# Weight splits of the expert stage pinned in order, and copies of results issued behind the next tile's split, on one Trainium2 core

## The chip, the cores and the metric

The program runs on one core of one Trainium2 chip. The metric is device microseconds of one execution. Three executions of the kernel before took 1781.1, 1781.54 and 1781.61 us; the median is 1781.54 us.

## What is computed

A two-layer trunk over 256 tokens of width 1024, in float32. Each layer has a token mixer (RWKV-7 beside latent attention) and a channel mixer: dense SwiGLU in layer 0, and in layer 1 the part that this change touches, a top-2-of-8 expert SwiGLU with hidden width 3584:

```python
def moe_swiglu(h, router_w, router_b, w1, w3, w2):
    logits = (h @ router_w).astype(jnp.float32) + router_b.astype(jnp.float32)
    top_v, top_i = lax.top_k(logits, TOP_K)
    probs = jax.nn.softmax(top_v, axis=-1)
    combine = jnp.sum(jax.nn.one_hot(top_i, N_EXPERTS, dtype=jnp.float32) * probs[..., None], axis=-2)
    out = jnp.zeros_like(h)
    for e in range(N_EXPERTS):
        out = out + combine[..., e:e + 1].astype(h.dtype) * swiglu(h, w1[e], w3[e], w2[e])
    return out
```

## The kernel before, in words

**Split numbers.** A product of float32 matrices is made of matmuls on rounded halves: a high part (`eh` of a weight tile, a copy on ACT, line 259) and the rest (`el`, a subtraction on DVE, line 264). Where an expert has many tokens ("large": experts 0, 2, 4, 6, 7 in the kernel's order) `mm3` makes three matmuls of each block: high by high, high by low, low by high (lines 347 to 349). The three "small" experts 1, 3 and 5 (`SMALL`) hold at most 64 tokens; both halves of the tokens then lie side by side in one stationary operand, and two matmuls do (lines 1871, 1872). Of one tile in each strip of a small expert only half is split; its other half goes in as plain float32 (line 1874).

**Strips and tiles.** Each expert's hidden width is cut into 7 strips of 512 (the loop `for f in range(nf)` in `experts`). A strip takes six weight tiles of 128x2048 (1024 KB each): two of w1, two of w3, and two of w2 that belong to the strip before, since the down projection runs one strip behind. The text calls them tile 1 to tile 6 of a strip. After tile 1 come the matmuls that turn the results of the strip before (`aT`, lines 1915 and 1925), for a small expert 16 of them.

**Lead.** `Tiles.take` is called as PE comes to a tile; it issues the high part of the tile three ahead and the low part of the tile two ahead. High parts have four buffers, low parts three, so the next high part can be written when PE is done with the tile before the present one, and a low part likewise. Raw weights have ten buffers in steady state (8 `er`, and `x0`, `x1`); a buffer is given back, and the load ten tiles on is issued by SP, when its low part is made.

**Results of a small strip.** `ea` and `eb` (lines 1899 and 1900) copy the two sums out of PSUM; `aT` adds their halves and turns them; `ez` takes silu on ACT (line 1917) and multiplies on DVE (line 1918); `ealo` holds the two parts of that product (ACT line 1921, DVE line 1922), which tiles 5 and 6 of the strip multiply.

**Side work.** `step` is called eight times in a strip. It pops one piece of `todo` (router, results of the expert before), or, at every third call, one of `slow`: the gathering of the next pair of experts' tokens (`find`, `norms`, eight `gather`, `back`). What is left at the end of a pair is issued in one go.

**Who sets the order.** The code is written in program order, but a scheduler at build time orders each engine's instructions by its own estimate; only what is wrapped in `keep_in_program_order` keeps its order among itself. Before, that holds for the `aT` matmuls and for silu (1902, 1917), and not for the splits or the copies. On the chip each engine goes through its list in order.

Of the kernel before, what the change touches and what calls it, by code (L numbers as in the profile page):

```python
# [223 lines left out]
class Tiles:  # L224
# [28 lines left out]
    def splits(self, upper, lower):  # L253
        nc = self.k.nc
        while self.upper < min(upper, len(self.tiles)):
            t = self.tiles[self.upper]
            self.load(self.upper + 1)
            t[4] = self.ppool.tile([128, 2048], F32R, name="eh", tag="eh", bufs=4)
            nc.scalar.activation(t[4][:, :t[2]], t[3][:, :t[2]], AF.Copy)  # L259
            self.upper += 1  # L260
        while self.lower < min(lower, len(self.tiles)):
            t = self.tiles[self.lower]
            t[5] = self.ppool.tile([128, 2048], F32R, name="el", tag="el", bufs=3)
            nc.vector.tensor_sub(t[5][:, :t[2]], t[3][:, :t[2]], t[4][:, :t[2]].bitcast(F32))  # L264
            if t[2] == 2048:
                self.used(self.lower)
            self.lower += 1
# [54 lines left out]
class K:  # L322
# [1501 lines left out]
    def step(self, n=1):  # L1824

        for _ in range(n):
            self.calls += 1
            if self.todo:
                self.todo.pop(0)()
            elif self.slow and (n > 1 or self.calls % 3 == 0):  # L1830
                self.slow.pop(0)()
# [29 lines left out]
    def experts(self, ws, small):  # L1861
# [3 lines left out]
        nf = DFE // 512  # L1865

        def mm(ps, e, x, w, start, stop):
            if e not in small:
# [7 lines left out]
        def up(e, f, behind):  # L1876
            x, hi, lo, selT, wsl = hg[e]
            hps, n = [], 0
            for w in ("moe_w1", "moe_w3"):
                ps = self.pshh.tile([128, 512], F32, name="ph", tag="p" + w)  # L1880
                for k0 in (0, 4):
                    blocks = ws.take((w, e, f))
                    for k in range(4):
                        if k % 2 == 0:
# [9 lines left out]
                    ws.taken()  # L1894
                hps.append(ps)
            a = self.ex.tile([128, 512], F32, name="ea", tag="ea", bufs=1)
            if e in small:
                b = self.ex.tile([128, 512], F32R, name="eb", tag="eahi", bufs=1).bitcast(F32)
                act.activation(a, hps[0], AF.Copy)
                act.activation(b, hps[1], AF.Copy)  # L1900
                return a, b
            tc.keep_in_program_order(act.activation(a, hps[0], AF.Silu))
# [3 lines left out]
        def turned(now, spare=False):  # L1906
            e, f, a = now
            pt = self.pg("aT")
            if e in small:

                for i in range(2):
                    for k in range(4):
                        o = i * 256 + k * 64
                        tc.keep_in_program_order(
                            pe.matmul(pt[:, o:o + 64], a[i][:, k * 128:k * 128 + 128], self.c("sum2"), start=True, stop=True))
                z = self.work.tile([128, T], F32, name="ez", tag="sq", bufs=3)
                tc.keep_in_program_order(act.activation(z, pt[:, :T], AF.Silu))
                v.tensor_mul(z, z, pt[:, T:])
                t = self.ex.tile([128, 512], F32R, name="ealo", tag="ealo", bufs=1)
                t4, z = t.rearrange("p (k i s) -> p k i s", k=4, i=2), z.rearrange("p (k s) -> p k s", k=4)  # L1920
                act.activation(t4[:, :, 0, :], z, AF.Copy)
                v.tensor_sub(t4[:, :, 1, :], z, t4[:, :, 0, :].bitcast(F32))
                return t
# [10 lines left out]

        def down(e, f, aT, py, then=None):
            selT, wsl = hg[e][3:]
            ends, last = f == nf - 1, e == NE - 1 and f == nf - 1
            for p in range(4):
                if p % 2 == 0:
                    blocks = ws.take(("moe_w2", e, f))  # L1940
                for j in range(2):
                    c, kk = (p // 2, p % 2 * 2 + j) if ends else (j, p)
                    sl = slice(kk * 128, kk * 128 + 128)
                    x = (aT[:, sl],) if e in small else (aT[0][:, sl], aT[1][:, sl])
                    mm(py[c], e, x, blocks[p % 2 * 2 + j], f == 0 and kk == 0, ends and kk == 3)
                if then and p == 0:
                    then[2] = turned(then, True)
                if ends and p == 1:
# [203 lines left out]
```

## Time and profile before

| what | value |
|---|---|
| median of three executions | 1781.54 us |
| the profiled execution | 1786.92 us, of which the span is 1785.1 us |
| PE busy | 1660.6 us (93%) |
| DVE busy | 1460.9 us (82%) |
| ACT busy | 1124.9 us (63%) |
| data moved | 501.94 MB, mean 281 GB/s |

The expert stage fills the time from about 758 us to the end. The table is an average over stages with different limits, so the stage must be read by itself: PE's idle time there, the clock granted to it, and what it waited for. A busy PE is not PE at its peak: at the slower clock level the same matmul takes longer and counts as busy.

### The profile page before, as it was taken

Reading aid. Unit: us, or ns where it says so; the run is one execution under the profiler, and the core shown is the slowest. Engines: PE = TensorE matmul, PEld = TensorE weight load, DVE = VectorE, ACT = ScalarE, POOL = GpSimd, SP = SyncE. Lnnn points to the kernel's source line nnn. Section 1 sums busy time; section 2 is a strip of 40 time slices with the busy share of each in tenths; the row PEclk is TensorE's granted clock in tenths of the full one; section 3 lists DMA queues with packets and bytes.
Section 4 is the critical chain, followed back from the end, with each engine's and each line's share of the span. In section 5 each row is a group of like instructions: output and inputs, shape, how many; then the busy total and the mean of one; then the engine's idle time right before and its main releaser. Section 6 shows DMA issues by size and latency. Waiting matters only on the chain.

```text
span 1785.1 us, 29101 instructions
## 1 busy us (share of the span) xinstructions
PE 1660.6 (93%) x10976; PEld 1425.7 (80%) x10976; DVE 1460.9 (82%) x2085; ACT 1124.9 (63%) x1481; POOL 6.6 (0%) x19
## 2 busy tenths in 40 slices
PE   5888999999999899899998999988999888999997
PEld 4877999999998799788776788666788666888885
DVE  6897787888769688788997799866998777988986
ACT  3655556555565455567776677756777666767674
POOL 0000000000000000000000000000000000000000
PEclk9998999999999799899999999998999988999999
DMA  8734466888533556969799999888999888999990
GB/s 275 248 114 152 152 212 202 302 290 289 193 120 124 179 184 230 374 252 365 268 420 383 356 354 358 330 326 333 351 369 355 313 337 338 349 364 348 358 354 26
DMA packets 92945, 501.94 MB, mean 281 GB/s; under 512 B 11498, under 2 KB 13034, under 8 KB 49788
## 3 DMA queue, kind: packets, MB, share of 16 engines
q1 hardware_dynamic: 91788, 498.54, 75.9%
q8 instruction: 88, 1.44, 0.3%
q10 hardware_dynamic: 720, 1.42, 0.2%
q14 instruction: 61, 0.50, 0.1%
q0 software_dynamic: 288, 0.03, 0.0%
HBM read 498.91 MB, written 1.05 MB: 280 GB/s over the span
## 4 chain that ended last, share of the span: by engine, by line
PE 76%; DVE 11%; ACT 4%; issue 4%; DMA 4%; ACTq 0%; DVEq 0%
PE ph L348 7%; PE ph L347 7%; PE ph L349 7%; PE pj L347 4%; PE pj L348 4%; PE pj L349 4%; DVE el L264 4%; PE py L348 3%; PE py L349 3%; PE py L347 3%; PE ph L1872 3%; ACT eh L259 3%; PE ph L1871 2%; PE psh L347 2%; PE psh L348 2%
## 5 line engine op out<-in xcount | busy, mean ns | idle before, releaser
L264 DVE TENSOR_TENSOR el<-er,eh 128x2048 fp32r<-128x2048 f32 (+1 forms) x268 | 589.9, 2222 | 107.4 <-ACT eh L259 94.2
L259 ACT ACTIVATE eh<-er 128x2048 fp32r<-128x2048 f32 (+1 forms) x268 | 490.5, 1860 | 41.1 <-PE ph L349 16.2
L341 ACT ACTIVATE wh<-wr 128x512 fp32r<-128x512 f32 (+1 forms) x366 | 222.9, 619 | 214.1 <-PE pj L348 62.2
L342 DVE TENSOR_TENSOR wl<-wr,wh 128x512 fp32r<-128x512 f32 (+1 forms) x366 | 242.8, 673 | 66.8 <-ACT wh L341 65.5
L347 PE MATMUL pj<-hhi,wh 128*128 128x256 f32 x704 | 208.7, 303 | 9.4 <-ACT hhi L469 7.8
L348 PE MATMUL pj<-hlo,wh 128*128 128x256 f32 x704 | 203.0, 290 | 0.5 <-DVE hlo L342 0.4
L349 PE MATMUL pj<-hhi,wl 128*128 128x256 f32 x704 | 202.7, 289 | 0.0
L264 DVE TENSOR_TENSOR el<-x,eh 128x2048 fp32r<-128x2048 f32 x66 | 144.7, 2204 | 17.4 <-ACT eh L259 15.1
L347 PEld LDWEIGHTS pj<-hhi,wh 128*128 128x128 f32 x704 | 136.7, 197 | 17.0 <-ACT hhi L469 9.2
L348 PEld LDWEIGHTS pj<-hlo,wh 128*128 128x128 f32 x704 | 138.5, 197 | 2.8 <-issue 1.1
L349 PEld LDWEIGHTS pj<-hhi,wl 128*128 128x128 f32 x704 | 138.4, 197 | 1.1 <-issue 0.6
L259 ACT ACTIVATE eh<-x 128x2048 fp32r<-128x2048 f32 x66 | 120.8, 1851 | 10.9 <-PE py L349 5.6
L348 PE MATMUL py<-el,eahi 128*128 128x512 f32 x272 | 106.8, 393 | 2.9 <-DVE el L264 2.8
L349 PE MATMUL py<-eh,ealo 128*128 128x512 f32 x272 | 106.1, 390 | 0.0
L347 PE MATMUL py<-eh,eahi 128*128 128x512 f32 x272 | 102.2, 390 | 0.0
L348 PE MATMUL psh<-xu,wh 128*128 128x258 f32 x336 | 95.3, 284 | 0.0
L347 PE MATMUL psh<-xu,wh 128*128 128x258 f32 x336 | 95.2, 283 | 0.0
L349 PE MATMUL psh<-xu,wl 128*128 128x258 f32 x336 | 94.9, 282 | 0.0
L347 PE MATMUL ph<-eh,hhi 128*128 128x512 f32 x224 | 90.4, 404 | 0.0
L348 PE MATMUL ph<-el,hlo 128*128 128x512 f32 x224 | 89.0, 397 | 1.5 <-DVE el L264 1.5
L348 PE MATMUL ph<-el,hhi 128*128 128x512 f32 x224 | 88.8, 397 | 1.0 <-DVE el L264 1.0
L384 DVE SCALAR_TENSOR_TENSOR wr<-wr,cB 128x1024 f32<-128x1024 f32 x64 | 77.9, 1220 | 14.1 <-DMA wr<-in_ada_w_dram 13.8
(470 smaller groups left out, 3679.4 us busy)
## 6 DMA issues: line engine op xcount, KB each, us to landing
er<-in_moe_w_dram SPq DMA_DIRECT2D x268, 1024.0 KB, 6.9
x<-in_moe_w_dram SPq DMA_DIRECT2D x66, 1024.0 KB, 6.8
wr<-in_ada_w_dram SPq DMA_DIRECT2D x64, 512.0 KB, 4.3
wr<-in_w_in_dram SPq DMA_DIRECT2D x52, 512.0 KB, 4.1
wr<-in_ffn_up_dram SPq DMA_DIRECT2D x44, 512.0 KB, 4.3
aw<-in_ada_w_dram SPq DMA_DIRECT2D x32, 512.0 KB, 4.8
wr<-in_ffn_w_dram SPq DMA_DIRECT2D x22, 512.0 KB, 4.4
wr<-in_w_o_dram SPq DMA_DIRECT2D x16, 512.0 KB, 4.5
```

Of the source, the lines that this page charges most:

```text
L259: nc.scalar.activation(t[4][:, :t[2]], t[3][:, :t[2]], AF.Copy)
L264: nc.vector.tensor_sub(t[5][:, :t[2]], t[3][:, :t[2]], t[4][:, :t[2]].bitcast(F32))
L341: self.nc.scalar.activation(hi, src, AF.Copy)
L342: self.nc.vector.tensor_sub(lo, src, hi.bitcast(F32))
L347: mm(out, whi, xhi, start=start, stop=False, skip_group_check=True)
L348: mm(out, whi, xlo, start=False, stop=False, skip_group_check=True)
L349: mm(out, wlo, xhi, start=False, stop=stop, skip_group_check=True)
L384: x = v.scalar_tensor_tensor(w, w, 1.0, self.cB, op0=OP.mult, op1=OP.mult, accum_out=mod[:, n:n + 1])
L1871: pe.matmul(ps, x[0], w[0], start=start, stop=False, skip_group_check=True)
L1872: pe.matmul(ps, x[0], w[1], start=False, stop=stop, skip_group_check=True)
```

## The change

1. The high and low splits of expert weights are pinned: they keep program order among themselves and against everything else that is pinned on ACT or DVE.
2. For small experts a list `after` is kept. The copies `ea` and `eb`, the silu with its product (`multiplied`), and the parts of the product (`parts`) are put on it, pinned, and one of them is issued at each take of a tile, behind that take's splits. The copy of the w1 sums is now issued by itself and not together with that of the w3 sums.
3. `step` takes a piece of the gathering at every fourth call, not every third.

```diff
-            nc.scalar.activation(t[4][:, :t[2]], t[3][:, :t[2]], AF.Copy)
+            self.k.tc.keep_in_program_order(nc.scalar.activation(t[4][:, :t[2]], t[3][:, :t[2]], AF.Copy))
...
-            nc.vector.tensor_sub(t[5][:, :t[2]], t[3][:, :t[2]], t[4][:, :t[2]].bitcast(F32))
+            self.k.tc.keep_in_program_order(
+                nc.vector.tensor_sub(t[5][:, :t[2]], t[3][:, :t[2]], t[4][:, :t[2]].bitcast(F32)))
...
-            elif self.slow and (n > 1 or self.calls % 3 == 0):
+            elif self.slow and (n > 1 or self.calls % 4 == 0):
...
+        after, pin = [], tc.keep_in_program_order
+        def then():
+            if after:
+                after.pop(0)()
...
                     blocks = ws.take((w, e, f))
+                    then()
...
+                if e in small:
+                    t = (self.ex.tile([128, 512], F32R, name="eb", tag="eahi", bufs=1).bitcast(F32) if w == "moe_w3" else
+                         self.ex.tile([128, 512], F32, name="ea", tag="ea", bufs=1))
+                    hps[-1] = t
+                    after.append(lambda t=t, ps=ps: [None, pin(act.activation(t, ps, AF.Copy))][0])
+            if e in small:
+                return hps
-            if e in small:
-                b = self.ex.tile([128, 512], F32R, name="eb", tag="eahi", bufs=1).bitcast(F32)
-                act.activation(a, hps[0], AF.Copy)
-                act.activation(b, hps[1], AF.Copy)
-                return a, b
...
-                z = self.work.tile([128, T], F32, name="ez", tag="sq", bufs=3)
-                tc.keep_in_program_order(act.activation(z, pt[:, :T], AF.Silu))
-                v.tensor_mul(z, z, pt[:, T:])
...
-                act.activation(t4[:, :, 0, :], z, AF.Copy)
-                v.tensor_sub(t4[:, :, 1, :], z, t4[:, :, 0, :].bitcast(F32))
+                def multiplied():
+                    z = self.work.tile([128, T], F32, name="ez", tag="sq", bufs=3)
+                    z4 = z.rearrange("p (k s) -> p k s", k=4)
+                    pin(act.activation(z, pt[:, :T], AF.Silu))
+                    pin(v.tensor_mul(z, z, pt[:, T:]))
+                    def parts():
+                        pin(act.activation(t4[:, :, 0, :], z4, AF.Copy))
+                        pin(v.tensor_sub(t4[:, :, 1, :], z4, t4[:, :, 0, :].bitcast(F32)))
+                    after.append(parts)
+                after.append(multiplied)
                 return t
...
                     blocks = ws.take(("moe_w2", e, f))
+                    then()
```

**ACT, the sixth strip of expert 1.** Ahead stands the order before, from the copy `ea` of the strip's w1 sums (`ph_11582`). The four `eh` rows between it and `eh_11659` belong to tiles 4, 5 and 6 of the same strip and tile 1 of the next; `eh_11659` of 128x1024 is the half split of tile 2, `eh_11673` is tile 3.

```order
L1899 ACTIVATE ea_11655<-ph_11582 128x512
L259 ACTIVATE eh_11583<-er_11439 128x2048
L1917 ACTIVATE ez_11608<-aT_11599 128x256
L259 ACTIVATE eh_11614<-er_11457 128x2048
L1921 ACTIVATE ealo_11611<-ez_11608 128x4x64
L259 ACTIVATE eh_11627<-er_11484 128x2048
L1900 ACTIVATE eb_11656<-ph_11626 128x512
L259 ACTIVATE eh_11641<-er_11486 128x2048
L259 ACTIVATE eh_11659<-er_11515 128x1024
L259 ACTIVATE eh_11673<-er_11528 128x2048
```

The same place in the order now, from the high part of the strip's tile 3 (`eh_11570`) on; tiles 4, 5 and 6 are `eh_11583`, `eh_11609` and `eh_11626`, tile 1 of the next strip is `eh_11642`.

```order
L259 ACTIVATE eh_11570<-er_11424 128x2048
L259 ACTIVATE eh_11583<-er_11440 128x2048
L259 ACTIVATE eh_11609<-er_11456 128x2048
L1933 ACTIVATE ez_11615<-aT_11599 128x256
L259 ACTIVATE eh_11626<-er_11484 128x2048
L1937 ACTIVATE ealo_11608<-ez_11615 128x4x64
L259 ACTIVATE eh_11642<-er_11486 128x2048
L1909 ACTIVATE ea_11624<-ph_11582 128x512
L259 ACTIVATE eh_11658<-er_11510 128x1024
L1909 ACTIVATE eb_11657<-ph_11625 128x512
```

Before, the copy of `ph_11582` stands ahead of the high parts of that strip's tiles 4, 5 and 6. Now it stands behind all of them and behind tile 1 of the next strip. On DVE the order of such a strip is the same in both programs.

**DVE, the router at the entry of the expert stage**, before: from the comparison of the logits (line 1637) on to the ranks and what is made of them.

```order
L1637 TENSOR_TENSOR cmp_9942<-cmp_9942,eq_9943 128x128
L1638 TENSOR_REDUCE rank_9937<-cmp_9942 128x16
L1639 TENSOR_SCALAR ind_9938<-rank_9937 128x16
L1659 TENSOR_SCALAR oh0_9967<-rank_9937 128x16
L1659 TENSOR_SCALAR oh1_9968<-rank_9937 128x16
```

And now (the lines have moved down by one):

```order
L1638 TENSOR_TENSOR cmp_9942<-cmp_9942,eq_9943 128x128
L343 TENSOR_TENSOR ht1_9499<-xgT_9847,ht0_9498 128x2x256
L265 TENSOR_TENSOR el_9908<-er_9878,eh_9902 128x2048
L265 TENSOR_TENSOR el_9912<-er_9880,eh_9904 128x2048
L1639 TENSOR_REDUCE rank_9937<-cmp_9942 128x16
L343 TENSOR_TENSOR rsh_9941<-rs_y_9921,rsh_9941 128x2
```

Two low parts now stand between the comparison and the ranks. Before, the first three low parts stood further up, among the last weight splits of the token mixer.

**DVE, the end of expert 0**, where the rest of the gathering is issued in one go (`hg` on the left of line 1789 is a gathered block in PSUM; line 1796 makes the two experts' low parts), before, from the half split of tile 2 of expert 1's first strip:

```order
L264 TENSOR_TENSOR el_10972<-x1_10729,eh_10952 128x1024
L264 TENSOR_TENSOR el_11035<-er_10757,eh_10970 128x2048
L1789 TENSOR_TENSOR hg_10915<-hg_10915,rsb_10548 128x192
L1789 TENSOR_TENSOR hg_10995<-hg_10995,rsb_10548 128x192
L1796 SCALAR_TENSOR_TENSOR hlo_10546<-hg_10915,mod11_7670,hlo_10546 128x64
L1796 SCALAR_TENSOR_TENSOR hlo_10546<-hg_10995,mod11_7670,hlo_10546 128x64
L1796 SCALAR_TENSOR_TENSOR hg_10547<-hg_10915,mod11_7670,hg_10547 128x128
L1796 SCALAR_TENSOR_TENSOR hg_10547<-hg_10995,mod11_7670,hg_10547 128x128
L264 TENSOR_TENSOR el_11051<-er_10784,eh_11033 128x2048
```

And now:

```order
L265 TENSOR_TENSOR el_10953<-x1_10713,eh_10933 128x1024
L1790 TENSOR_TENSOR hg_10914<-hg_10914,rsb_10548 128x192
L1797 SCALAR_TENSOR_TENSOR hlo_10546<-hg_10914,mod11_7670,hlo_10546 128x64
L1790 TENSOR_TENSOR hg_10976<-hg_10976,rsb_10548 128x192
L1797 SCALAR_TENSOR_TENSOR hg_10547<-hg_10914,mod11_7670,hg_10547 128x128
L1797 SCALAR_TENSOR_TENSOR hlo_10546<-hg_10976,mod11_7670,hlo_10546 128x64
L1797 SCALAR_TENSOR_TENSOR hg_10547<-hg_10976,mod11_7670,hg_10547 128x128
L1790 TENSOR_TENSOR hg_10995<-hg_10995,rsb_10548 128x192
L1797 SCALAR_TENSOR_TENSOR hlo_10546<-hg_10995,mod11_7670,hlo_10546 128x64
L1790 TENSOR_TENSOR hg_10976<-hg_10976,rsb_10548 128x192
L1797 SCALAR_TENSOR_TENSOR hg_10547<-hg_10995,mod11_7670,hg_10547 128x128
```

Five gathers are left at this place where three were, and no split stands among them.

## Rows read from the trace of the kernel before

**Rows 1.** The page: span, busy time and count of instructions of each engine, and in 40 slices the clock granted to PE (tenths of full speed) and the busy share of the DMA engines.

```profile
span 1785.1 us, 29101 instructions
PE 1660.6 (93%) x10976; PEld 1425.7 (80%) x10976; DVE 1460.9 (82%) x2085; ACT 1124.9 (63%) x1481; POOL 6.6 (0%) x19
...
PEclk9998999999999799899999999998999988999999
DMA  8734466888533556969799999888999888999990
```

**Rows 2.** Busy time by stretch, core 0, cut at the start of each strip's `aT` matmuls in expert 1, with two strips at the edges of experts 3 and 5. Columns: the stretch, its length, busy us (x instructions) of PE, PEld, DVE, ACT, POOL, granted clock, DMA share, GB/s.

```profile
898.41:915.37 16.96, 16.29 (x83) 12.75 (x82) 16.09 (x18) 13.05 (x13) 0.00 (x0) 1.00 1.01 421
915.37:929.01 13.64, 13.64 (x65) 10.73 (x64) 13.64 (x9) 12.20 (x10) 0.00 (x0) 1.00 1.01 419
929.01:943.67 14.66, 13.64 (x64) 10.54 (x63) 12.17 (x9) 10.04 (x9) 0.00 (x0) 1.00 1.01 419
943.67:962.31 18.64, 15.77 (x65) 11.49 (x64) 13.07 (x9) 11.84 (x10) 0.00 (x0) 0.91 1.01 418
962.31:981.47 19.16, 15.77 (x65) 11.57 (x64) 12.87 (x9) 11.84 (x10) 0.00 (x0) 0.91 0.89 338
981.47:1000.99 19.52, 16.85 (x69) 12.20 (x68) 13.91 (x9) 14.13 (x11) 0.00 (x0) 0.91 0.90 340
1142.92:1162.07 19.15, 16.75 (x82) 12.33 (x81) 16.69 (x17) 12.88 (x11) 0.00 (x0) 1.00 0.85 335
1495.02:1515.39 20.37, 17.91 (x69) 13.49 (x68) 14.06 (x9) 14.26 (x11) 0.00 (x0) 0.83 0.87 321
```

**Rows 3.** The same view over whole small experts (four strips of expert 1, six each of experts 3 and 5), and over parts of large ones.

```profile
929.01:1000.99 71.98, 62.02 (x260) 45.80 (x259) 52.01 (x33) 47.86 (x40) 0.00 (x0) 0.93 0.95 376
1142.92:1257.99 115.07, 98.23 (x406) 71.92 (x405) 82.46 (x57) 74.29 (x62) 0.00 (x0) 0.91 0.88 333
1400.16:1515.39 115.23, 98.04 (x405) 72.06 (x404) 82.60 (x57) 74.46 (x62) 0.00 (x0) 0.91 0.88 333
...
1300.00:1400.00 100.00, 98.61 (x461) 80.50 (x460) 88.40 (x77) 73.29 (x67) 0.00 (x0) 1.00 0.93 352
1700.00:1720.00 20.00, 20.00 (x91) 16.46 (x90) 17.78 (x11) 15.14 (x10) 0.00 (x0) 1.00 0.96 360
```

**Rows 4.** ACT in order of time in expert 1's sixth strip: start, length, line, operation, count, and in brackets the idle time before and who ended it.

```profile
966.94 0.60 ACT L1899 ACTIVATE ea<-ph 128x512 f32<-128x512 f32 x1 [6.09 <-PE ph L1874]
967.43 1.90 ACT L259 ACTIVATE eh<-er 128x2048 fp32r<-128x2048 f32 x1
```

**Rows 5.** PE in order of time behind it.

```profile
969.39 0.50 PE L1871 MATMUL ph<-eh,hlo 128*128 128x512 f32 x1 [0.63 <-ACT eh L259]
971.72 0.79 PE L1872 MATMUL ph<-el,hlo 128*128 128x512 f32 x1 [1.82 <-DVE el L264]
972.31 0.63 PE L1871 MATMUL ph<-eh,hlo 128*128 128x512 f32 x1
972.74 0.63 PE L1872 MATMUL ph<-el,hlo 128*128 128x512 f32 x1
...
975.01 0.39 PE L1872 MATMUL py<-el,ealo 128*128 128x512 f32 x1
975.24 0.40 PE L1871 MATMUL py<-eh,ealo 128*128 128x512 f32 x1
...
979.76 0.50 PE L1872 MATMUL ph<-el,hlo 128*128 128x512 f32 x1 [0.93 <-DVE el L264]
```

**Rows 6.** ACT in order of time in expert 1's third strip, the one of 13.64 us.

```profile
918.04 1.91 ACT L259 ACTIVATE eh<-er 128x2048 fp32r<-128x2048 f32 x1 [0.36 <-PE ph L1871]
919.99 0.60 ACT L1899 ACTIVATE ea<-ph 128x512 f32<-128x512 f32 x1
920.49 0.41 ACT L1921 ACTIVATE ealo<-ez 128x256 fp32r<-128x256 f32 x1
921.43 2.90 ACT L259 ACTIVATE eh<-er 128x2048 fp32r<-128x2048 f32 x2 [0.54 <-ACT ealo L1921]
```

**Rows 7.** Groups of instructions by shape in 943.67 to 1000.99 us: line, engine, operation, names, shape, count, busy us, mean ns of one, idle before and who ended it.

```profile
L264 DVE TENSOR_TENSOR el<-er,eh 128x2048 fp32r<-128x2048 f32 x14 | 31.9, 2287 | 17.5 <-ACT eh L259 17.4
L259 ACT ACTIVATE eh<-er 128x2048 fp32r<-128x2048 f32 x14 | 26.4, 1904 | 0.0
...
L1922 DVE TENSOR_TENSOR ealo<-ez,ealo 128x256 fp32r<-128x256 f32 x3 | 1.3, 417 | 0.0
```

**Rows 8.** The waits of the whole run: who waited for whom, us in total, times, longest.

```profile
ACT ea L1899 <- PE ph L1874: 81.7, 14, 7.4
```

**Rows 9.** The same for the DMA queue's own waits, which is SP's.

```profile
SPq L246 <- DVE el L264: 478.7, 205, 22.7
```

**Rows 10.** The page's issues of DMAs: count, KB each, median us from issue to landing.

```profile
er<-in_moe_w_dram SPq DMA_DIRECT2D x268, 1024.0 KB, 6.9
```

**Rows 11.** DVE in order of time at the entry of the expert stage.

```profile
739.50 2.28 DVE L264 TENSOR_TENSOR el<-er,eh 128x2048 fp32r<-128x2048 f32 x1
741.70 0.41 DVE L416 TENSOR_TENSOR sqs<-sqs,sq 128x256 f32<-128x256 f32 x1
742.04 0.47 DVE L750 SCALAR_TENSOR_TENSOR xT<-pj,hg,xT 128x256 f32<-128x256 f32 x1
...
748.93 0.29 DVE L1637 TENSOR_TENSOR cmp<-cmp,eq 128x128 f32<-128x128 f32 x1
749.26 0.29 DVE L1638 TENSOR_REDUCE rank<-cmp 128x16 f32<-128x128 f32 x1
```

**Rows 12.** DVE in order of time at the end of expert 0: two gathers.

```profile
879.95 0.62 DVE L1789 TENSOR_TENSOR hg<-hg,rsb 128x192 f32<-128x192 f32 x2
880.69 0.55 DVE L1796 SCALAR_TENSOR_TENSOR hlo<-hg,mod,hlo 128x64 fp32r<-128x64 f32 x2
881.41 0.62 DVE L1796 SCALAR_TENSOR_TENSOR hg<-hg,mod 128x128 fp32r<-128x128 f32 x2 [0.17 <-ACT hg L1795]
```

More of the change, by code (lines that the diff above doesn't have):

```diff
@@ L1915, in turned @@
                             pe.matmul(pt[:, o:o + 64], a[i][:, k * 128:k * 128 + 128], self.c("sum2"), start=True, stop=True))
-                z = self.work.tile([128, T], F32, name="ez", tag="sq", bufs=3)
-                tc.keep_in_program_order(act.activation(z, pt[:, :T], AF.Silu))
-                v.tensor_mul(z, z, pt[:, T:])
                 t = self.ex.tile([128, 512], F32R, name="ealo", tag="ealo", bufs=1)
-                t4, z = t.rearrange("p (k i s) -> p k i s", k=4, i=2), z.rearrange("p (k s) -> p k s", k=4)
-                act.activation(t4[:, :, 0, :], z, AF.Copy)
-                v.tensor_sub(t4[:, :, 1, :], z, t4[:, :, 0, :].bitcast(F32))
+                t4 = t.rearrange("p (k i s) -> p k i s", k=4, i=2)
+                def multiplied():
[8 more added lines that the diff above has]
+                after.append(multiplied)
                 return t
@@ L1933, in turned, with down @@
             return ahi, alo
-        def down(e, f, aT, py, then=None):
+        def down(e, f, aT, py, other=None):
             selT, wsl = hg[e][3:]
@@ L1945, in down @@
                     mm(py[c], e, x, blocks[p % 2 * 2 + j], f == 0 and kk == 0, ends and kk == 3)
-                if then and p == 0:
-                    then[2] = turned(then, True)
+                if other and p == 0:
+                    other[2] = turned(other, True)
                 if ends and p == 1:
```

## The prediction, written before the changed kernel ran

> **What bounds the kernel now.** Read the page first: PE is busy for 93% of the span, but the clock line has 9s in its right half, where the expert stage lies, and the DMA line 9s and 8s there [rows 1]. So PE, the DMA engines and a wait are all candidates, and the stage must be cut up. The second view is busy time by stretch, one strip to a row. In large experts PE is busy for 20.00 of 20 us at full clock, although DMA runs at 360 GB/s [rows 3]: PE bounds them, and nothing there can be gained by order. In small experts a strip takes 18.6 to 19.5 us, PE is busy for some 15.8 of it, DVE for 13, ACT for 12, the clock is 0.91 and DMA moves 338 GB/s [rows 2]. No engine is full. Yet the third strip of expert 1, with the same work, took 13.64 us at clock 1.00, and DMA moved 419 GB/s [rows 2]. The loss of some 5 us per strip is a wait.
>
> The third view, the engines in order of time, names it. ACT sat idle for 6.09 us until the plain matmuls of tile 2 ended, then made the copy `ea`, and only then the high part of tile 4 [rows 4]. PE, through with tile 3, waited 0.63 us for that high part and 1.82 us for the low part that DVE made of it; later 0.93 us more [rows 5]. And the matmuls behind those gaps start 0.43 us apart (972.31, 972.74), those further on 0.23 (975.01, 975.24) [rows 5]: the lower clock level, 1.2 GHz instead of 2.4. The wait of `ea` for line 1874 happened 14 times, 81.7 us in all [rows 8]. Buffers for three more high parts were free meanwhile, but ACT goes through its list in order, and `ea` stood in front.
>
> **The change, part by part.**
>
> *Copies behind the splits.* Now `ea` stands behind the high parts of tiles 4, 5, 6 and the next tile 1. In the strip of 13.64 us the order was nearly that: `ea` stood behind tile 6's high part, and did not hold ACT up [rows 6]. That strip is my model, and I ask what is late next in it. PE's four tiles from tile 3 to tile 6 are 32 matmuls at 0.23 us, 7.3 us. Between the end of tile 2 and that of tile 6 DVE must make the low part of tile 5, the product's part, the low parts of tile 6 and of the next tile 1: 3 x 2.29 + 0.42 = 7.3 us [rows 7], a little less where splits follow each other directly (31.9 us for 14 is 2.28 each). So DVE is level with PE, and I take 13.9 us, not 13.64, per strip; the strip before the change of expert holds a first tile of a large expert with four matmuls more, 0.9 us, so 14.8; the first strip of a small expert has the old expert's results to fold in and DVE busy for over 16 us, so 17, as 16.96 shows [rows 2]. ACT has five high parts at 1.9 us and a half one, and 2 us of copies, 11.8 of 13.9: free.
>
> The sum, from the stretches of whole experts [rows 3]: expert 1, 71.98 - (3 x 13.9 + 14.8) = 15.5; expert 3, 115.07 - (17 + 4 x 13.9 + 14.8) = 27.7; expert 5, 115.23 - 87.4 = 27.8. Together 71 us. Bounds: with 13.64 per strip 4 us more, and 2 more if the first strips take 16; with half of each loss coming back as another wait, 35.
>
> *Waits that pinning adds.* `ea` now waits behind a high part that needs PE to be done with tile 3; its reader, `aT`, comes four tiles later, 7 us. `eb` follows a half split and has two tiles. Silu and the parts stand behind high parts whose buffers PE frees before `aT` ends or just after tile 2. The readers of the parts come with tile 5. I cost these at nothing; their cover is the tiles named, and without it each would cost one tile, 1.8 us.
>
> *Loads.* SP's list of loads is unchanged, and SP is released by low parts: 205 waits for DVE [rows 9]. A faster strip therefore asks for its loads sooner: 6 x 1.049 MB in 13.9 us is 453 GB/s, more than the 418 to 421 that the saturated rows show [rows 2]. At 419 a strip's loads take 15.0 us, so the queue falls behind by 1.1 us a strip, 7.7 us over seven. A load has nine tiles, 20.8 us, between its issue and its split, and lands in 6.9 [rows 10]: 13.9 us of room. It fits; cost nothing, bound below.
>
> The Trainium skill (DMA: Bandwidth & Descriptors, section "Where 436 GB/s comes from") says that for loads from HBM the memory's share of about 358 GB/s per core binds and not the ports; that would give 17.6 us per strip and speaks against this change. The rows differ: 418 to 421 GB/s stood for four strips, 64 us, with no other core of the chip in use by this program.
>
> *Entry.* Two low parts of 2.29 us now stand between the comparison (748.93) and the ranks (749.26) [rows 11], on the chain router, places, gather, first matmul: 4.5 us. The old place at 739.50 held up the last residual sums until 742.04, though PE was just done: some 1.3 us come back. The third low part moves behind the gathers, 2.3 us, half of it hidden. So 4.5 us lost; bounds 2 and 7.
>
> *Gathers at every fourth place.* Expert 0 is left with two gathers more to issue at once. A pair holds DVE for 0.62 + 0.55 + 0.62 = 1.8 us [rows 12]; the same work leaves the strips before, which PE bounds. I take 1.5 us lost, bounds -1 and +4. In the later large experts 48 calls less the results' six give ten pieces of 13 or 11: the gathers nearly all fit.
>
> *Large experts.* PE bounds them; pinning can only add. Per strip DVE has six low parts and three short results, 15 of 16.9 us. I cost it at nothing; see the last rival.
>
> Sum: 71 - 4.5 - 1.5 = 65 us. The profiled execution took 1786.92 us and would take 1721.9; the median of the runs is 5.4 us below the profiled one, so **1716.5 us** against 1781.54. With the bounds of the small terms, 1702 to 1732.
>
> **The rivals.**
>
> *A new wait in the small strips.* DVE is level with PE by my own count, and any late high part shows in full, with the lower clock behind it. For: DVE was busy for 13.64 of 13.64 us in the model strip [rows 2]. Against: the next strip, 14.66, ran into the old order again, not into DVE. At 16 us a strip, fifteen strips lose 2.1 each, 32 us: 1748.
>
> *The loads.* If DMA holds only 365 GB/s, about what it moves in large experts (352 to 360 [rows 3]), a strip takes 17.2 us. Expert 1 would use up its room and lose 9, experts 3 and 5 some 18 each, since large strips of 16.9 to 18 us hardly refill it: 45 us back, 1761. For: the DMA share is 0.93 and 0.96 there, near full. Against: SP waited for buffers in those rows, and the same queue gave 419 when asked. The skill's 358 would end in the same place.
>
> *Slower.* One mechanism: in a large strip a pinned low part stands before a short result that PE needs, or behind one that waits, and comes one split late. The price is 2.2 us in each of 35 large strips, 77 us, against 65 gained: 1793. It decides from 1.9 us a strip. Against: low parts run two tiles ahead, 5.5 us there.
>
> That the change does not do what it says can be left out: the order shows `ea` moved.
>
> **How the numbers follow.** My forecast has 0.70, the new wait 0.15, the loads 0.10, slower 0.04, other small outcomes 0.01. The range is the forecast's own 1702 to 1732, widened to 1750 to take in most of the new-wait case; it leaves out the loads, the slower case and a tail on either side, 2 in 10. About 0.2% (3.6 us) is what a measurement of this kernel can tell from no change. Faster takes the first three cases less a part of the loads, 0.94; no change 0.02; slower 0.04.
>
> **What would show it.** Right: the wait of `ea` for line 1874 gone from the list of waits; small strips of 13.6 to 14.5 us at clock 1.00 with DMA near 419 GB/s; PE's waits for low parts in the middle of small strips gone; the ranks some 4.5 us after the comparison. Wrong: a wait of `eh` for a load (loads), DVE without idle time and PE waiting for it in small strips (new wait), PE idle in large strips (slower), or small strips still at 18 us.

## The result, and the profile after

The changed kernel took 1729.19 us, median of three executions (1725.53 to 1730.41), against 1781.54 us. The ratio is 0.9702, with a 95% interval of 0.9679 to 0.9725. The profiled execution took 1730.41 us, its span is 1728.6 us; the profile before had 1785.1 [rows 1]. Forecast were 1716.5 us and a range of 1702 to 1750. All medians and ratios here leave out one slow execution, of the run pins (4078.94 us).

Start with the page again: busy time of the engines, the clock granted to PE and the DMA share in 40 slices.

```profile
span 1728.6 us, 29096 instructions
PE 1631.4 (94%) x10976; PEld 1411.1 (82%) x10976; DVE 1461.1 (85%) x2085; ACT 1123.6 (65%) x1481; POOL 6.6 (0%) x19
...
PEclk9999999999989999989999999999999999999998
DMA  8725466788733556868979999989999899999980
```

The work is the same (PE 10976 matmuls, DVE and ACT busy for as long as before). PE is busy for 29 us less with the same matmuls: more of them ran at the higher clock (1.00 in the small strips below, 0.91 in [rows 2]). The other 27 us were idle time of PE.

The busy time by stretch, cut at the same places as before: expert 1's six strips, then the first and a middle strip of expert 3, then whole small experts (the last four strips of expert 1, all six of experts 3 and 5), then a piece of a large one. Columns: the stretch, its length, busy us (x instructions) of PE, PEld, DVE, ACT, POOL, granted clock, DMA share, GB/s.

```profile
906.91:926.14 19.23, 16.62 (x82) 12.59 (x81) 17.36 (x18) 14.70 (x14) 0.00 (x0) 1.00 0.90 346
926.14:939.86 13.72, 13.72 (x65) 10.73 (x64) 13.72 (x9) 11.99 (x11) 0.00 (x0) 1.00 0.99 388
939.86:953.57 13.71, 13.71 (x65) 10.73 (x64) 13.18 (x9) 11.96 (x11) 0.00 (x0) 1.00 0.96 383
953.57:966.93 13.36, 13.36 (x64) 10.62 (x63) 12.64 (x9) 11.77 (x10) 0.00 (x0) 1.00 1.01 420
966.93:980.52 13.59, 13.59 (x65) 10.81 (x64) 12.90 (x9) 11.82 (x11) 0.00 (x0) 1.00 1.01 421
980.52:995.02 14.50, 14.50 (x69) 11.56 (x68) 13.81 (x9) 12.74 (x11) 0.00 (x0) 1.00 1.01 419
1137.61:1157.83 20.22, 17.79 (x81) 13.64 (x80) 18.10 (x18) 14.49 (x13) 0.00 (x0) 0.92 0.85 333
1171.43:1185.01 13.58, 13.58 (x65) 10.81 (x64) 12.88 (x9) 11.82 (x11) 0.00 (x0) 1.00 1.00 416
...
939.86:995.02 55.16, 55.16 (x260) 43.72 (x259) 52.53 (x33) 48.29 (x40) 0.00 (x0) 1.00 1.00 411
1137.61:1226.69 89.08, 86.65 (x406) 68.44 (x405) 83.50 (x58) 74.49 (x62) 0.00 (x0) 0.98 0.95 383
1369.39:1458.42 89.03, 86.59 (x405) 68.42 (x404) 83.13 (x58) 74.46 (x62) 0.00 (x0) 0.98 0.95 383
1660.00:1680.00 20.00, 20.00 (x91) 16.50 (x90) 17.77 (x10) 15.04 (x11) 0.00 (x0) 1.00 0.97 377
```

Read it against [rows 2, 3]. The strips of 18.6 to 19.2 us are strips of 13.4 to 13.7 now, the last strip of expert 1 went from 19.52 to 14.50, PE is busy all through them, and the clock column says 1.00. The last four strips of expert 1 went from 71.98 to 55.16 us, experts 3 and 5 from 115.07 and 115.23 to 89.08 and 89.03. The first strips had no part in the gain: 19.23 against 16.96 in expert 1, 20.22 against 19.15 in expert 3.

ACT in order of time in the strip at 1171.43 shows why, beside [rows 4]:

```profile
1175.92 0.40 ACT L1937 ACTIVATE ealo<-ez 128x256 fp32r<-128x256 f32 x1
1177.72 1.92 ACT L259 ACTIVATE eh<-er 128x2048 fp32r<-128x2048 f32 x1 [1.40 <-issue]
1179.55 0.58 ACT L1909 ACTIVATE ea<-ph 128x512 f32<-128x512 f32 x1
```

`ea` waits for nothing: the plain matmuls of tile 2 that it needs (now line 1882) ended 3.5 us before it starts. It stands behind a high part, where before it stood in front of one and waited for 6.09 us. For the 1.40 us that ACT waits before that high part the profile names no releaser; PE has no idle time in this strip. No wait of `ea` for line 1882, the old line 1874 of [rows 8], is left in the list.

Now the two places where time was lost. DVE at the entry, to be read beside [rows 11], and then in the first strip of expert 3:

```profile
749.88 0.29 DVE L1638 TENSOR_TENSOR cmp<-cmp,eq 128x128 f32<-128x128 f32 x1
...
750.69 4.48 DVE L265 TENSOR_TENSOR el<-er,eh 128x2048 fp32r<-128x2048 f32 x2
755.09 0.28 DVE L1639 TENSOR_REDUCE rank<-cmp 128x16 f32<-128x128 f32 x1
...
1146.85 2.28 DVE L265 TENSOR_TENSOR el<-er,eh 128x2048 fp32r<-128x2048 f32 x1
1149.04 0.41 DVE L1934 TENSOR_TENSOR ez<-ez,aT 128x256 f32<-128x256 f32 x1
1149.38 0.87 DVE L2008 SCALAR_TENSOR_TENSOR xT<-sct,mod,xT 128x256 f32<-128x256 f32 x2
1150.16 0.41 DVE L1938 TENSOR_TENSOR ealo<-ez,ealo 128x256 fp32r<-128x256 f32 x1
```

Two low parts stand between comparison and ranks, as forecast. In the first strip silu ended at 1142.50, but its product `ez` stands behind low parts and additions to xT and comes at 1149.04. ACT (first row) waits for it, and PE (second row) for what comes of it:

```profile
1149.49 0.42 ACT L1937 ACTIVATE ealo<-ez 128x256 fp32r<-128x256 f32 x1 [5.19 <-DVE ez L1934]
1150.62 0.50 PE L1879 MATMUL py<-eh,ealo 128*128 128x512 f32 x1 [2.05 <-DVE ealo L1938]
```

**Where the 56.5 us of span went.** From the first `aT` of expert 0 to the last `aT` of the stage: 980.29 us before (779.04 to 1759.33), 917.85 after (785.00 to 1702.85), 62.4 less. From the comparison to the first `aT`: 30.11 before, 35.12 after, 5.0 more. The comparison itself began 0.95 us later (749.88 against 748.93). 62.4 - 5.0 - 0.95 = 56.5.

### The profile page after: what moved, and what is told of

Its sections match the earlier page's. It is cut to its first block, busy times and chain, and to the rows that moved or that the text cites. A ratio compares the mean times of both kernels' runs of the same rounds, so it can differ in the third digit from the quotient of the medians.

```text
span 1728.6 us, 29096 instructions
## 1 busy us (share of the span) xinstructions
PE 1631.4 (94%) x10976; PEld 1411.1 (82%) x10976; DVE 1461.1 (85%) x2085; ACT 1123.6 (65%) x1481; POOL 6.6 (0%) x19
## 4 chain that ended last, share of the span: by engine, by line
PE 80%; DVE 10%; DMA 4%; issue 3%; ACT 2%; DVEq 0%; SPq 0%; ACTq 0%
PE ph L348 7%; PE ph L349 7%; PE ph L350 7%; PE pj L348 4%; PE pj L349 4%; PE pj L350 4%; PE py L349 4%; PE py L350 4%; PE ph L1880 3%; PE ph L1879 3%; PE py L348 3%; PE psh L348 2%; PE psh L349 2%; PE psh L350 2%; DVE el L265 2%
## 5 line engine op out<-in xcount | busy, mean ns | idle before, releaser
L265 DVE TENSOR_TENSOR el<-er,eh 128x2048 fp32r<-128x2048 f32 (+1 forms) x268 | 586.1, 2220 | 26.1 <-ACT eh L259 14.9
L385 DVE SCALAR_TENSOR_TENSOR wr<-wr,cB 128x1024 f32<-128x1024 f32 x64 | 78.0, 1219 | 17.6 <-DMA wr<-in_ada_w_dram 17.5
```

The costliest lines, as they stand in the source:

```text
L385: x = v.scalar_tensor_tensor(w, w, 1.0, self.cB, op0=OP.mult, op1=OP.mult, accum_out=mod[:, n:n + 1])
```

## The experiments

"Stage" is the time from the first `aT` to the last, "entry" from the comparison to the first `aT`, "strip" a middle strip of expert 3. Ratios are against the kernel before, run on the same chip.

| run | median us | ratio, 95% interval | entry | strip | stage |
|---|---|---|---|---|---|
| before | 1781.54 | 1 | 30.11 | 18.6 to 19.5 | 980.29 |
| changed | 1729.19 | 0.9702, 0.9679 to 0.9725 | 35.12 | 13.58 | 917.85 |
| again | 1727.04 | 0.9694, 0.9665 to 0.9723 | 35.19 | 13.59 | 917.63 |
| copies | 1731.96 | 0.9718, 0.9690 to 0.9745 | 29.81 | 14.85 | 926.43 |
| pins | 1814.44 | 1.0178, 1.0145 to 1.0210 | 35.19 | 20.4 | 1002.97 |
| eaonly | 1754.50 | 0.9839, 0.9815 to 0.9862 | 35.17 | 15.46 | 947.60 |
| prodonly | 1787.53 | 1.0025, 1.0005 to 1.0045 | 34.96 | 18.4 to 20.4 | 984.19 |
| fourth | 1788.12 | 1.0031, 1.0011 to 1.0051 | 30.15 | 18.4 to 19.4 | 982.51 |
| third | 1726.72 | 0.9703, 0.9677 to 0.9728 | 35.16 | 13.58 | 918.57 |
| raw5 | 1740.50 | 0.9775, 0.9749 to 0.9800 | 35.86 | 13.6 to 15.3 | 928.22 |
| both | 1722.59 | 0.9663, 0.9646 to 0.9680 | 30.34 | 13.59 | 916.52 |
| spread | 1716.85 | 0.9632, 0.9610 to 0.9655 | 30.35 | 13.58 | 913.33 |
| best | 1717.45 | 0.9642, 0.9607 to 0.9677 | 30.74 | 13.58 | 910.74 |

**Copies moved, splits not pinned (copies).**

```diff
-            self.k.tc.keep_in_program_order(nc.scalar.activation(t[4][:, :t[2]], t[3][:, :t[2]], AF.Copy))
+            nc.scalar.activation(t[4][:, :t[2]], t[3][:, :t[2]], AF.Copy)
...
-            self.k.tc.keep_in_program_order(
-                nc.vector.tensor_sub(t[5][:, :t[2]], t[3][:, :t[2]], t[4][:, :t[2]].bitcast(F32)))
+            nc.vector.tensor_sub(t[5][:, :t[2]], t[3][:, :t[2]], t[4][:, :t[2]].bitcast(F32))
```

> The changed kernel with the two pins on the expert weights' splits taken back; copies, silu and parts stay behind the next tile's split, gathers stay at every fourth place. Theory (the copy of the w1 product at the head of ACT's row was the block, and moving the copies alone takes it away): the strips of the small experts stay at 13.6 us, and the entry, where two low parts now run ahead of the rank, gets its 6 us back, so 1729 - 6 = about 1723 us. Rival (the splits have to be held in order for the copies to fall behind them): strips back at 17 to 19 us, 1760 to 1785 us.

The entry came back in full, 29.81 us. The strips did not stay at 13.6: 14.85. So the theory holds for the larger part (53.9 of the 62.4 us of the stage) and fails for a smaller one. DVE in order of time in a strip of this run shows it; the last row is PE's, in order of time:

```profile
1185.05 2.29 DVE L264 TENSOR_TENSOR el<-er,eh 128x2048 fp32r<-128x2048 f32 x1
1187.26 0.42 DVE L1933 TENSOR_TENSOR ez<-ez,aT 128x256 f32<-128x256 f32 x1
...
1190.83 0.42 DVE L1937 TENSOR_TENSOR ealo<-ez,ealo 128x256 fp32r<-128x256 f32 x1
...
1191.30 0.50 PE L1878 MATMUL py<-eh,ealo 128*128 128x512 f32 x1 [0.94 <-DVE ealo L1937]
```

Silu ended at 1184.40, but a low part had been moved ahead of the product. With pins the product came 0.5 us after silu (1173.75 to 1174.26). The pins on the splits thus hold the product's place: 8.6 us over the stage, of which the entry takes 5 back. By their times alone this kernel and the changed one cannot be told apart.

**Splits pinned, copies not moved (pins).** The kernel before with the two pins alone; the diff is the one above with its signs turned.

> The kernel before with the two pins on the splits alone: copies, silu and parts at their old place, gathers at every third place. In a strip of a small expert the copy of the w1 product then stands behind the splits of tiles 3 and 4 but ahead of those of tiles 5 and 6. Theory (how far the splits are ahead when ACT stops is what counts): tile 5 is split from the end of tile 2 on, copy 0.6 + part 0.4 + high part 1.9 + low part 2.3 = 5.2 us against 4.5 us of matmuls of tiles 3 and 4, so 0.7 to 1.5 us are lost a strip over the 15 strips that follow a first one: 1729 + 10 to 22, less 4 for the gathers, is 1735 to 1750 us. Rival (the copies' own move is the cause, the pins only cost): 1781 + 6 at the entry = about 1787 us.

Both theories missed: 1814 us, slower than before by 1.8%. The copy of the w1 sums had not fallen behind tile 4's high part, as the expectation took it to have; ACT stands at it for 6.00 us as before. What changed is what the scheduler then did with PE's matmuls. ACT (one row) and PE in order of time:

```profile
1220.38 0.60 ACT L1900 ACTIVATE ea<-ph 128x512 f32<-128x512 f32 x1 [6.00 <-PE ph L1875]
...
1222.83 0.50 PE L1872 MATMUL ph<-eh,hhi 128*128 128x512 f32 x1 [0.63 <-ACT eh L259]
1225.81 1.22 PE L1872 MATMUL py<-eh,ealo 128*128 128x512 f32 x2 [2.47 <-ACT eh L259]
1226.83 0.64 PE L1873 MATMUL ph<-el,hhi 128*128 128x512 f32 x1
```

Two matmuls of tile 5 (`py`) stand in the middle of tile 4 (`ph`), wait there for tile 5's high part, and hold up seven matmuls of tile 4. This wait came 12 times, 28.0 us. A pin also moves what is not pinned.

**One of the two groups moved (eaonly, prodonly).** With the splits pinned, only the two result copies stay behind the splits, or only silu, product and parts.

The first diff is that of eaonly, the second that of prodonly.

```diff
-                    pin(act.activation(z, pt[:, :T], AF.Silu))
-                    pin(v.tensor_mul(z, z, pt[:, T:]))
+                    act.activation(z, pt[:, :T], AF.Silu)
+                    v.tensor_mul(z, z, pt[:, T:])
-                    def parts():
-                        pin(act.activation(t4[:, :, 0, :], z4, AF.Copy))
...
-                    after.append(parts)
+                    act.activation(t4[:, :, 0, :], z4, AF.Copy)
...
-                after.append(multiplied)
+                multiplied()
```

```diff
-                    after.append(lambda t=t, ps=ps: [None, pin(act.activation(t, ps, AF.Copy))][0])
             if e in small:
+                for t, ps in zip(hps, pss):
+                    act.activation(t, ps, AF.Copy)
                 return hps
```

> The changed kernel with silu, product and the product's two parts back where they were (emitted with aT, not pinned); the two copies of the results stay behind the next tile's split and the splits stay pinned. Theory (the copy of the w1 product was the block; silu and parts have a whole tile of slack at either place): strips of 13.6 to 14.9 us, 1729 to 1748 us. Rival (silu and the parts in front of a split block ACT as much as the copy did): strips of 16 us or more, 1765 us or more.

> The changed kernel with the two copies of the results back in one place at the end of the w3 product and not pinned; silu, product and parts stay behind the next tiles' splits, the splits stay pinned. It is the fourth corner beside the changed kernel (13.6 us a strip), the run eaonly (15.5) and the run pins (20.4). Theory (each of the two waits stops ACT by itself: the copy of the w1 product costs 4 to 5 us a strip, silu's wait for aT 1.9 us): strips of 17.5 to 19 us, 1729 + 15 x 4 to 5.4 us = 1789 to 1810 us. Rival (the two waits overlap, and one of them gone is most of the gain): 15 to 16 us, 1750 to 1765 us.

With the copies alone a strip takes 15.46 us, between the two theories. ACT in order of time in that run:

```profile
1174.88 0.38 ACT L1933 ACTIVATE ez<-aT 128x256 f32<-128x256 f32 x1 [3.84 <-PE aT L1926]
1175.16 1.91 ACT L259 ACTIVATE eh<-er 128x2048 fp32r<-128x2048 f32 x1
```

Silu now stops ACT in front of a high part until `aT` is done: 20 times, 70.0 us in all. It costs 1.9 us a strip: PE waits there for two low parts, 0.46 and 0.32 us, and is busy for 14.59 us instead of 13.58 at the same granted clock of 1.00; where this 1.0 us arises was not followed further. With silu and parts alone moved, the wait of the w1 copy is back and the strip takes 18.4 to 20.4 us, longer than the 17.5 to 19 expected, although the run as a whole (1787.53 us) came out just below the time expected. The list of waits of that run, to be read beside [rows 8]:

```profile
ACT ea L1912 <- PE ph L1882: 83.3, 14, 7.4
```

So there are four corners with the splits pinned. The stage takes 1003.0 us with neither group moved (gathers at every third place there, which is worth nothing in the changed kernel, see third), 984.2 with the product's, 947.6 with the copies', 917.9 with both. The copy of the w1 sums was the block; silu stood behind it as a second one of about half the price (29.7 us of the stage, against 66.3). The Trainium skill (PSUM — Partial Sum Buffer, section "Engine vs sequencer instructions") says that ScalarE's queue is strict first in, first out; both waits agree, 6.09 us in [rows 4] and 3.84 us here, each with a high part right behind it that starts without a wait of its own.

**Gathers (fourth, third).** The kernel before with `self.calls % 4`, and the changed one with `self.calls % 3`, one character each.

> The kernel before with gathers at every fourth place instead of every third, nothing else. Theory (the gathers' place matters only where they run out into the border between experts 0 and 1): the border grows by about 4 us, nothing else moves: 1782 to 1787 us. Rival (a quarter fewer gathers in front of DVE's low parts gives expert 0 its time back): expert 0 shorter by 1 to 3 us and no longer border, 1778 to 1781 us.

> The changed kernel with gathers at every third place again. Theory: the border between experts 0 and 1 and the strip behind it get back the 4.2 and 2.3 us by which they grew, or most of it, and expert 0 loses its 1.7 us: 1729 - 3 to 5 = 1724 to 1726 us. Rival (the border is longer because of the pinned low parts, not of the number of gathers that are left): 1728 to 1731 us.

Compare expert 0 with the border and expert 1's first strip: before 136.33 us (779.04 to 915.37), fourth 140.30 (778.51 to 918.81), after 141.14, third 140.00 (779.75 to 919.75). In the kernel before, the later gathers cost 4.0 us there, as expected, and 2.2 us of the whole stage (982.51 against 980.29). In the changed kernel earlier gathers give back 1.1, not 4 to 6, and the stage as a whole nothing (918.57 against 917.85). The rival of the second run is right by these stretches (its median, 1726.72, lies between the two forecasts): with pinned splits the stretch is longer at either place of the gathers. The run pins, with the gathers at every third place and the copies where they were, takes 140.50 there (787.55 to 928.05). So the pins alone cost some 4 us, the later gathers alone cost some 4 us, and the two do not add up. Which pinned instruction is at fault, these runs do not say; in the run both, with the first three splits free, it is still 140.02.

**Room for the loads (raw5).**

```diff
-RAW = 8
+RAW = 5
```

> The changed kernel with 5 buffers of its own for raw weights instead of 8, so that a load has 6 tiles instead of 9 between its issue and its split: 6 x 2.27 - 6.9 = 6.7 us of room against a lag of 1.1 us a strip. Theory of the prediction (the room covers a queue that is behind by 1.1 us a strip): expert 1 as now, the last one or two strips of experts 3 and 5 lose some 1 us each, 1729 + 0 to 5 us. Rival (the 9 tiles are needed, because a load takes longer than 6.9 us when the queue is full): strips of small experts go to 15 us (6.29 MB at 419 GB/s) from the third strip on, 11 strips x 1.4 us = 15 us: about 1744 us, with waits of the high part for a load in the list.

The truth lay between. The stretches of expert 3's fourth and fifth strips in that run, with the columns of above:

```profile
1182.93:1198.21 15.28, 14.19 (x66) 10.65 (x64) 13.05 (x8) 11.67 (x10) 0.00 (x0) 1.00 1.01 421
1198.21:1213.18 14.97, 14.20 (x65) 10.65 (x64) 13.09 (x8) 12.09 (x11) 0.00 (x0) 1.00 1.01 419
```

One row of ACT in the fifth; the high parts behind it wait in the same way (46 such waits in the run, 26.1 us):

```profile
1199.32 1.92 ACT L259 ACTIVATE eh<-er 128x2048 fp32r<-128x2048 f32 x1 [0.58 <-DMA er<-in_moe_w_dram]
```

Experts 3 and 5 kept 13.6 us up to the third strip, and the fourth and fifth took 15.0 to 15.5: 6.29 MB at 419 GB/s are 15.0 us. The room exists and is used up, but sooner than I reckoned. A strip of 13.59 us falls behind by 1.4 us, not 1.1, and a load lands later the fuller the queue is. The page's DMA issues, asked for 1171 to 1226 us of the changed kernel, give 14.7 us from issue to landing, against 6.9 over the whole run before [rows 10]:

```profile
er<-in_moe_w_dram SPq DMA_DIRECT2D x21, 1024.0 KB, 14.7
```

With six tiles, 6 x 2.27 = 13.6 us, that does not fit. With nine it does, but the median hides how closely: between 1171 and 1231 us the landing climbs from 6.7 to 18.7 us. Here is one load of the changed kernel near the end of expert 3, as SP issues it, its time to landing, and the high part that ACT makes of it:

```profile
1209.60 0.33 SPq L246 DMA_DIRECT2D x<-in_moe_w_dram  x1
DMA to landing us min/median/max: 16.4/16.4/16.4
1226.88 1.91 ACT L259 ACTIVATE eh<-x 128x2048 fp32r<-128x2048 f32 x1
```

From issue to split it has 17.3 us, not 9 x 2.27 = 20.4, and it lands 0.9 us before it is needed. The closest load of expert 5 (issued at 1441.34, landed after 16.5, split at 1458.62) has 0.7 us. So no strip of the changed kernel waits for a load, but at the end of experts 3 and 5 it is less than 1 us from doing so; runs with 6 or 7 buffers were not made.

**Versions beyond the change (both, spread), and the changed kernel once more beside the last one (again, best).** In both, the first three splits are not pinned and the gathers are at every third place. spread also puts the four pieces `back` at every second call; best does that only before expert 1 and the large experts.

The first diff is that of both, the second that of spread against both; best has `self.spaced = 0 if e in (2, 4) else 4`.

```diff
+            x = nc.scalar.activation(t[4][:, :t[2]], t[3][:, :t[2]], AF.Copy)
+            if self.upper > 2:
+                self.k.tc.keep_in_program_order(x)
...
+            if self.lower > 2:
+                self.k.tc.keep_in_program_order(x)
...
-            elif self.slow and (n > 1 or self.calls % 4 == 0):
+            elif self.slow and (n > 1 or self.calls % 3 == 0):
```

```diff
             if self.todo:
-                self.todo.pop(0)()
+                if n > 1 or len(self.todo) != self.spaced or self.calls % 2 == 0:
+                    self.todo.pop(0)()
+                    self.spaced = min(self.spaced, len(self.todo)) if self.spaced else 0
...
                     self.todo.append(lambda kk=kk: back(e, kk, y, selT))
+                self.spaced = 4
```

> The changed kernel with gathers at every third place again and with the first three splits of the expert stage unpinned. Theory (two pinned low parts between comparison and ranks are the 6 us by which the entry grew, and the gathers' place is worth 4 or less): first aT at 779 instead of 785, 1726.7 - 6 = 1720 to 1721 us. Rival (the low parts have to be made before the first matmul at any place, so the entry takes as long): 1726 to 1727 us.

> The kernel of the run labelled both, with the four pieces that add an expert's results to xT put at every second place of the next expert's strips instead of at four places in a row. Theory (in the first strip of a small expert DVE is full, 17.6 of 20.2 us and the low parts late because of eight additions of 0.48 us; two of the four move into the next strip, where DVE has 0.8 us idle): the first strips of experts 3 and 5 go from 20.2 to 18.5 to 19.5 us and the second ones from 13.6 to 14.3, 1719 to 1721 less 1 to 2 us = 1718 to 1720 us. Rival (PE's own 17.8 us there and the strip behind it, where DVE is as full, give nothing): the same as both within 1 us; or 2 us slower, if the pieces collide with the product's parts.

> The changed kernel once more, beside the next run on one chip. The stages before the experts took 740 to 752 us in the profiled executions so far, by the clock; from the comparison to the first aT every kernel with the pins took 35.1 to 35.9 us and every one without 29.8 to 30.4. Expected: 1727 to 1731 us, 35.1 us from the comparison to the first aT, 917.9 us from there to the last aT.

> The kernel of the run spread, with the results put at every second place only where the next expert is expert 1 or a large one, since in experts 3 and 5 the first strip took 20.35 us with it and 19.14 without. Theory: first strips of experts 3 and 5 back at 19.1 us, 2 x 1.2 us less than spread, 911 us from the first aT to the last instead of 913.3, about 1714 to 1716 us, and some 13 us less than the changed kernel beside it. Rival (what spread gained came from the earlier stages' clock alone, 770 us to the first aT against 775): as the run both, 916.5 us from the first aT to the last, 1720 us or more.

Unpinning three splits gives the entry back (30.34 against 30.11 before), so the pins of the first splits are its cause. The run spread gained, but not where it was meant to: in the first strips of experts 3 and 5 PE waits for `ealo` as long as before. The gain lies in expert 1's first strip, 17.08 us for 19.23, and where a small expert gives way to a large one. Two stretches there, of again and then of best:

```profile
984.69:1008.73 24.04, 23.88 (x116) 19.54 (x114) 20.71 (x17) 15.42 (x13) 0.00 (x0) 1.00 1.01 420
1008.73:1019.10 10.37, 9.85 (x49) 7.67 (x48) 9.25 (x10) 8.29 (x6) 0.00 (x0) 1.00 1.01 417
```

```profile
988.46:1002.49 14.03, 14.03 (x71) 11.85 (x70) 11.27 (x8) 8.85 (x9) 0.00 (x0) 1.00 1.01 421
1002.49:1021.49 19.00, 19.00 (x93) 15.59 (x92) 18.43 (x17) 13.14 (x10) 0.00 (x0) 1.00 1.01 419
```

That is 34.4 us against 33.0, and so at all three such places; expert 1's second strip gives 0.5 us back (14.19 in spread, 13.71 in both). best stands at 19.13 us in the first strips of experts 3 and 5 where spread had 20.35, as expected in size, but the reason is not shown: both runs have the same wait there (2.07 and 2.08 us), and only the granted clock differs (1.00 and 0.92). From the comparison to the last `aT` again takes 952.8 us, both 946.9, spread 943.7, best 941.5. So by this stretch spread and best beat the changed kernel. By the whole run spread's interval lies below both of the changed kernel's, while that of best (up to 0.9677) overlaps the one of again (from 0.9665); between spread and best the medians tell nothing.

## Why the prediction was right, and where it was off

**What bounds, and the block: right.** The wait named in advance was the main cause: with everything else of the change in place, putting the copies back costs 66 us of the stage (prodonly, 984.2 against 917.9), and moving copies, silu and parts without the pins brings 53.9.

**Small strips: right in sum, wrong in two sizes.** Forecast 71 us, measured 16.8 + 26.0 + 26.2 = 69.0. The middle strips were better than 13.9, PE fills them, and DVE has 0.7 us idle of 13.58; so PE and not DVE binds. The first strips of experts 3 and 5 were put at 17 us and took 20.2. That the sum is so near is luck: the other strips gave 4.4 us more than forecast, the two first strips 6.4 us less. The model for them was expert 1's 16.96 [rows 2], a strip of the old order; in the new one it takes 19.23 itself. The step that failed is "DVE busy for over 16 us, so 17": busy time says nothing of the order, and the product stands behind three low parts and four additions. Nor was there a block to take away: before, `ea` did not wait in that strip of 19.15 us:

```profile
1149.14 0.58 ACT L1899 ACTIVATE ea<-ph 128x512 f32<-128x512 f32 x1
```

PE's idle time in it is 2.4 us before (19.15 - 16.75) and after (20.22 - 17.79); the 1.1 us more come with the granted clock, 0.92 against 1.00.

**Entry: right.** 5.0 us against 4.5. The 1.3 us that were to come back ahead of the comparison cannot be seen: there the profiled executions differ by more than that (last section).

**Gathers: mis-sized.** Forecast 1.5 us with a bound of 4, measured 4.8 (141.14 against 136.33). By fourth the gathers alone make 4.0 in the kernel before, but by third they are worth 1.1 in the changed one, and the pins alone make as much (pins, 140.50). The term that was missing is a cost of the pins at this border.

**Loads: right in the outcome, by a margin that was luck.** The forecast left 13.9 - 7.7 = 6.2 us of room. Landing climbed from 6.7 to 18.7 us around the end of expert 3, by 12 us and not 7.7, and issue to split is 17.3 us there and not 20.8; 0.9 us was left, and 0.7 in expert 5. The rate held: 416 to 421 GB/s where the queue is full. The Trainium skill (DMA: Bandwidth & Descriptors, section "Where 436 GB/s comes from") names about 358 GB/s as what binds; the measurement decides against it for one core by itself. The rival of the loads was wrong in its rate and a near one all the same: raw5 waits for loads at 419 GB/s, for want of buffers, with a price of 10 us.

**Waits that pinning adds, and large strips: right for this change only.** PE waits for nothing new in middle strips. In the first strips of experts 3 and 5 it does: the product that was put behind the next splits comes so late that ACT waits 5.19 us and PE 2.05, where the prediction put this term at nothing. The product's moved place is enough for that, without the pins on the splits: the run copies has the same wait (2.07 and 2.05 us), and in eaonly, where silu, product and parts stayed at their old place, PE waits for them nowhere. The large experts 2, 4, 6 and 7 lost 1.7 us in all, not 77. But the cost of a pin is not nothing by itself: without the moved copies the pins made the kernel slower by some 33 us. My slower rival had the place wrong (large strips); the case nearest to it sits in the small ones.

**The sum and the conversion.** Forecast 65 us off the profiled execution, measured 56.5. The 8.5 between them: small strips 2.0, entry 0.5, gathers 3.3, large experts and expert 1's second strip 1.8, the time before the comparison 0.95. The step from the profiled execution to the median was 5.4 us before and is 1.2 after, which makes 4.2 more; together they are the 12.7 us by which 1716.5 was too low. This last step is chance, since it depends on which execution was profiled. The ends 1702 and 1732 do not follow from the bounds beside the terms: those of entry and gathers give 1711.5 to 1721.5, with the strips' 6 us more 1705.5, and half of each loss coming back some 1752. By the bounds of the small terms 1729 lies outside; the end of 1732, which the working does not give, covers it. One reading is loose, without weight in the sum: as ACT's wait begins, tiles 1, 2 and 3 hold three of the four buffers for high parts, so one was free then, a second from the end of tile 1 and a third only for the last 2 us.

## What to carry to other kernels

Where an engine that works through its list in order waits for a result that nobody needs soon, look at what stands behind it: the price is the lateness of that work, and moving the waiting instruction behind work that can run was most of the cure here (53.9 of 62.4 us of the stage). Ask then what the moved instructions come too late for: in the first strips they did. An order held by pins is a whole: half of it can be worse than none, because the scheduler moves what is left free. Compare kernels by stretches between fixed instructions, since the profiled executions of one kernel can differ by more than a small edit is worth (10.4 us here).

## What the runs showed that I had not expected

- The same kernel in two profiled executions (changed and again) reached the comparison at 749.88 and 739.50 us, 10.4 us apart, and took 917.85 and 917.63 us for the stage behind the first `aT`. Over eleven further traces the comparison began between 739 and 752 us. In those two the whole difference thus lies before the experts; a difference of 5 us between medians needs the stretches beside it.
- The same wait in the first strip of experts 3 and 5 has two prices. In the run copies PE waits there for `ealo` for 2.07 us in expert 3 and 2.05 in expert 5; here are the two stretches, with the columns of above:

```profile
1133.23:1152.38 19.15, 16.48 (x82) 12.39 (x81) 16.69 (x17) 13.97 (x12) 0.00 (x0) 1.00 0.80 317
1367.09:1387.34 20.25, 17.82 (x81) 13.66 (x80) 17.73 (x18) 14.59 (x13) 0.00 (x0) 0.92 0.88 338
```

The granted clock fell behind the second wait and not behind the first, and the strip is 1.1 us longer. prodonly has it the other way round, 20.22 us in expert 3 and 19.13 in expert 5. The runs do not show what decides.
